# Softmax over 32,768 columns: five unequal pieces scaled on two engines, and a first load that ends in sixteen narrow transfers

## The chip, the cores and the metric

The kernel runs on one core of a Trainium2 chip. The metric is the device time of one execution in microseconds. The kernel before takes 2512.25 us, the median of three runs (2511.07 to 2513.49).

## The reference

A softmax over the last axis of a float32 tensor of 16 x 256 x 32768 (4096 rows of 32,768 columns, 537 MB in and as much out), with temperature 1.0:

```python
scaled = logits / temperature
scaled = scaled - scaled.max(axis=-1, keepdims=True)
exp_scaled = np.exp(scaled)
return exp_scaled / exp_scaled.sum(axis=-1, keepdims=True)
```

## The kernel before

Each row is cut into two halves of 16,384 columns, and the halves are laid on neighbouring partitions. A tile is 128 such half rows: 64 KB on each partition, 8.4 MB. There are 64 tiles and three tile buffers in one SBUF tensor `xs` (tile g uses buffer g mod 3). Every element is read from HBM once and written once.

All data moves through one queue, issued by SyncE (SP). `transfers` (L61) writes the order out by hand. "L" is a load and "S" a store of a tile: loads of tiles 0, 1 and 2; store 0 and load 3, each in two halves; stores 1 and 2; then for every following tile its load and the store of the tile before; at the end the loads of tiles 62 and 63, the stores of 61 and 62, and the last store in quarters. SP waits before a load until the store that last used the buffer has landed (L211), and before a store until the tile is scaled (L220). A transfer once issued stands in the queue behind those before it.

The work on one tile is in `compute` (L120). It cuts the tile into K = 4 pieces of `_PIECE` = 4096 columns. For each piece:

- VectorE takes the negative maximum of the piece per partition into a column of `t` (L133).
- ScalarE replaces the piece by exp(x - piece maximum) and adds up the exponentials into another column of `t` (L146).

Then come the small steps on 128 x 8 elements: VectorE swaps neighbouring partitions so that each half row sees the figures of the other half (L157), takes the maximum of the row (L161); ScalarE computes the factors exp(piece maximum - row maximum) into `ee` (L168); VectorE sums the row (L174) and takes the reciprocal (L186). At last VectorE multiplies each piece in place by its factor and the reciprocal in one instruction (L193), and the tile can be stored. The small tensors `t`, `ee`, `junk` and `row` exist twice (tile parity), so that VectorE waits, before it begins a tile, for the small steps of the tile before the last.

`Stream.wait` and `Stream.done` (L24, L34) set waits and increments of the engines; `Lanes.add` (L49) gives transfers their semaphores.

Of the kernel before, what the change touches and what calls it, by code (L numbers as in the profile page):

```python
# [7 lines left out]

_W = 16384
_BUFS = 3  # L10
_PIECE = 4096
_LAST_STORE = 4096


class Stream:


    def __init__(self, nc, engine, name):
        self.engine = engine
        self.sem = nc.alloc_semaphore(name)  # L20
        self.count = 0
        self.seen = {}
# [38 lines left out]
def transfers(n):  # L61
    half = _W // 2
    whole = [(0, _W)]
    halves = [(0, half), (half, half)]
    quarters = [(s, _LAST_STORE) for s in range(0, _W, _LAST_STORE)]
    plan = [("L", 0, whole), ("L", 1, whole), ("L", 2, whole)]
    plan += [("S", 0, halves), ("L", 3, halves), ("S", 1, whole), ("S", 2, whole)]
    for i in range(4, n - 2):
        plan += [("L", i, whole), ("S", i - 1, whole)]
    plan += [("L", n - 2, whole), ("L", n - 1, whole)]  # L70
    plan += [("S", n - 3, whole), ("S", n - 2, whole), ("S", n - 1, quarters)]
    return plan


@with_exitstack
def kernel(
    ctx: ExitStack,
    tc: tile.TileContext,
    logits: bass.AP,
    temperature: bass.AP,  # L80
    out: bass.AP,
):
    nc = tc.nc
    inv_t = 1.0 / float(temperature)
    P = nc.NUM_PARTITIONS
    fp32 = mybir.dt.float32
    Exp = mybir.ActivationFunctionType.Exp
    A = mybir.AluOpType

    xf = logits.flatten_outer_dims()  # L90
    of = out.flatten_outer_dims()
    N, V = xf.shape
    assert V == 2 * _W and (N * 2) % P == 0
    x = xf.rearrange("n (h v) -> (n h) v", h=2)
    o = of.rearrange("n (h v) -> (n h) v", h=2)
    G = N * 2 // P
    K = _W // _PIECE
    swap = [i ^ 1 for i in range(32)]

    ctx.enter_context(tc.tile_critical())  # L100
    X = nc.alloc_sbuf_tensor("xs", [P, _BUFS * _W], fp32)
    T = [nc.alloc_sbuf_tensor(f"t{q}", [P, 4 * K], fp32) for q in range(2)]
    E = [nc.alloc_sbuf_tensor(f"ee{q}", [P, 2 * K], fp32) for q in range(2)]
    J = [nc.alloc_sbuf_tensor(f"junk{q}", [P, 2 * K], fp32) for q in range(2)]
    R = [nc.alloc_sbuf_tensor(f"row{q}", [P, 4], fp32) for q in range(2)]

    sp = Stream(nc, nc.sync, "sp")
    dve = Stream(nc, nc.vector, "dve")
    act = Stream(nc, nc.scalar, "act")
    loads = Lanes(nc, "ld")  # L110
    stores = Lanes(nc, "st")
    landed = {}
    stored = {}
    scaled = {}
    hist = {}

    def overlapping(parts, s, n):
        return [token for (a, m), token in parts.items() if a < s + n and s < a + m]

    def compute(g):  # L120
        base = (g % _BUFS) * _W
        t, e, j_, r = T[g % 2], E[g % 2], J[g % 2], R[g % 2]
        tv = t[:, 0 : 4 * K].rearrange("p (a b k) -> p a b k", a=2, b=2)
        old = hist.get(g - 2)
        if old:
            dve.wait(*old)
        sums = None
        for k in range(K):
            s = k * _PIECE
            xs = X[:, base + s : base + s + _PIECE]  # L130
            dve.wait(*overlapping(landed[g], s, _PIECE))
            m = dve.done(
                nc.vector.tensor_reduce(  # L133
                    out=t[:, k : k + 1], in_=xs, axis=mybir.AxisListType.X, op=A.max, negate=True
                )
            )
            if inv_t != 1.0:
                dve.wait(m)
                m = dve.done(
                    nc.vector.tensor_scalar_mul(  # L140
                        out=t[:, k : k + 1], in0=t[:, k : k + 1], scalar1=inv_t
                    )
                )
            act.wait(m)
            sums = act.done(
                nc.scalar.activation(  # L146
                    out=xs,
                    in_=xs,
                    func=Exp,
                    bias=t[:, k : k + 1],  # L150
                    scale=inv_t,
                    accum_out=t[:, K + k : K + k + 1],
                )
            )
        dve.wait(sums)
        sh = dve.done(
            nc.vector.stream_shuffle(out=t[:, 2 * K : 4 * K], in_=t[:, 0 : 2 * K], mask=swap)  # L157
        )
        dve.wait(sh)
        mx = dve.done(  # L160
            nc.vector.tensor_reduce(  # L161
                out=r[:, 0:1], in_=tv[:, :, 0, :], axis=mybir.AxisListType.XY, op=A.min
            )
        )
        act.wait(mx)
        ev = e[:, 0 : 2 * K].rearrange("p (a k) -> p a k", a=2)
        ee = act.done(
            nc.scalar.activation(  # L168
                out=ev, in_=tv[:, :, 0, :], func=Exp, bias=r[:, 0:1], scale=-1.0
            )  # L170
        )
        dve.wait(ee)
        tr = dve.done(
            nc.vector.tensor_tensor_reduce(  # L174
                out=j_[:, 0 : 2 * K].rearrange("p (a k) -> p a k", a=2),
                in0=ev,
                in1=tv[:, :, 1, :],
                scale=1.0,
                scalar=0.0,
                op0=A.mult,  # L180
                op1=A.add,
                accum_out=r[:, 1:2],
            )
        )
        dve.wait(tr)
        rc = dve.done(nc.vector.reciprocal(out=r[:, 2:3], in_=r[:, 1:2]))  # L186
        dve.wait(rc)
        scaled[g] = {}
        for k in range(K):
            s = k * _PIECE  # L190
            xs = X[:, base + s : base + s + _PIECE]
            scaled[g][s, _PIECE] = dve.done(
                nc.vector.tensor_scalar(  # L193
                    out=xs,
                    in0=xs,
                    scalar1=e[:, k : k + 1],
                    scalar2=r[:, 2:3],
                    op0=A.mult,
                    op1=A.mult,
                )  # L200
            )
        hist[g] = (ee, tr)

    for what, g, parts in transfers(G):
        base = (g % _BUFS) * _W
        rows = slice(g * P, (g + 1) * P)
        if what == "L":
            landed[g] = {}
            for k, (s, n) in enumerate(parts):
                if g >= _BUFS:  # L210
                    sp.wait(*overlapping(stored[g - _BUFS], s, n))  # L211
                landed[g][s, n] = loads.add(
                    (g % _BUFS, k),
                    nc.sync.dma_start(out=X[:, base + s : base + s + n], in_=x[rows, s : s + n]),
                )
            compute(g)
        else:
            stored[g] = {}
            for k, (s, n) in enumerate(parts):
                sp.wait(*overlapping(scaled[g], s, n))  # L220
                stored[g][s, n] = stores.add(
                    (g % _BUFS, k),
                    nc.sync.dma_start(out=o[rows, s : s + n], in_=X[:, base + s : base + s + n]),  # L223
                )
    sp.wait(*stores.tokens())
# [35 lines left out]
```

## Time and profile before

| | |
|---|---|
| median of 3 runs | 2512.25 us |
| profiled execution | 2513.76 us |
| its span, first to last instruction | 2512.0 us |
| VectorE busy | 1755.7 us (70%) |
| ScalarE busy | 993.5 us (40%) |
| the transfer queue: share of 16 DMA engines' span | 99.8% |
| read from and written to HBM | 536.87 MB each |
| mean rate over the span | 427 GB/s |

The span is what the profile's views cover; 1.8 us of the execution lie outside it. DVE is VectorE, ACT is ScalarE, SPq the queueing of transfers by SyncE. The share of the queue adds up the durations of all packets; a packet is what one of the 16 DMA engines moves for one row of a transfer, 64 KB for a load or store of a whole tile. Engine idle times are named with what released the engine.

### The profile page before, as it was taken

The page shows a single profiled execution, that of the slowest core. Times are in us where ns is not written, and L with a number is a line of the kernel's source. Part 1 is how long each engine was busy: PE and PEld are TensorE (multiplying, and loading weights), DVE is VectorE, ACT ScalarE, POOL GpSimd, SP SyncE. Part 2 cuts the span into 40 slices and gives each one's busy share as a digit, 9 for nine tenths or more (in the row PEclk, how much of TensorE's full clock was granted, in tenths as well). Part 3 has the DMA queues.
Part 4 walks back from the last instruction along what each step waited for, and adds up shares of the span by engine and source line. Part 5 has one row for each costly group of instructions (what it writes and reads, how often), then busy time and mean ns, then how long its engine had stood idle before and what let it go on. Part 6 is the DMA issues. An engine that isn't in the chain of part 4 may idle for free.

```text
span 2512.0 us, 1661 instructions
## 1 busy us (share of the span) xinstructions
DVE 1755.7 (70%) x896; ACT 993.5 (40%) x577; POOL 0.2 (0%) x4
## 2 busy tenths in 40 slices
DVE  5866676766767667677676766777767676676776
ACT  3443342433424334243342433424334244342443
POOL 0000000000000000000000000000000000000000
DMA  9999999999999999999999999999999999999999
GB/s 409 443 427 432 434 432 432 425 432 432 420 433 425 429 431 422 432 424 430 433 421 431 434 427 425 434 431 422 433 432 421 431 422 433 433 420 432 434 420 389
DMA packets 19165, 1073.86 MB, mean 427 GB/s; under 512 B 2128, under 2 KB 2128, under 8 KB 2128
## 3 DMA queue, kind: packets, MB, share of 16 engines
q1 hardware_dynamic: 19152, 1073.75, 99.8%
q14 instruction: 13, 0.11, 0.0%
HBM read 536.87 MB, written 536.87 MB: 427 GB/s over the span
## 4 chain that ended last, share of the span: by engine, by line
DMA 57%; DVE 36%; ACT 5%; SPq 0%; issue 0%
DMA xs<-in_logits_dram 56%; DVE t L133 23%; DVE xs L193 12%; ACT xs L146 5%; DMA out_dram<-xs 1%; ACT ee L168 0%; SPq L223 0%; DVE row L186 0%; DVE row L161 0%; DVE t L157 0%; DVE junk L174 0%; DVE row L174 0%; SPq L256 0%; SPq L100 0%
## 5 line engine op out<-in xcount | busy, mean ns | idle before, releaser
L146 ACT ACTIVATE xs<-xs,t 128x4096 f32<-128x4096 f32 x256 | 949.2, 3708 | 1464.4 <-DVE t L133 1464.4
L133 DVE TENSOR_REDUCE t<-xs 128x1 f32<-128x4096 f32 x256 | 1113.4, 4412 | 462.1 <-DMA xs<-in_logits_dram 462.1
L193 DVE TENSOR_SCALAR xs<-xs,ee,row 128x4096 f32<-128x4096 f32 x256 | 600.4, 2409 | 2.3
L157 DVE LOAD_MASK_SELECT t<-t x64 | 0.9, 14 | 248.1 <-ACT xs L146 248.1
L146 ACT ACTIVATION_READ_ACCUMULATOR xs<-xs,t 128x1 f32 x256 | 47.7, 186 | 0.0
L168 ACT ACTIVATE ee<-t,row 128x8 f32<-128x8 f32 x64 | 19.2, 301 | 27.6 <-DVE row L161 27.6
L174 DVE CUSTOM_DVE_ANT_1 junk<-ee,t 128x8 f32<-128x8 f32 x64 | 10.7, 167 | 23.6 <-ACT ee L168 23.6
L186 DVE RECIPROCAL row<-row 128x1 f32<-128x1 f32 x64 | 10.5, 164 | 2.2
L161 DVE TENSOR_REDUCE row<-t 128x1 f32<-128x8 f32 x64 | 10.3, 161 | 2.2
L157 DVE STREAM_SHUFFLE t<-t 128x8 f32<-128x8 f32 x64 | 10.2, 160 | 0.0
L174 DVE DVE_READ_ACCUMULATOR2_ANT row<- 128x1 f32 x64 | 5.3, 83 | 0.0
L146 ACT ACT_TABLE_LOAD x1 | 1.3, 1283 | 0.9 <-SPq L100 0.9
L242 POOL MEMSET const-bfloat16-1.0<- 128x1 bf16 x1 | 0.1, 101 | 0.0
L242 POOL MEMSET const-uint8-127<- 128x1 uint8 x1 | 0.1, 101 | 0.0
L242 POOL MEMSET const-float32-0.0<- 128x1 f32 x1 | 0.1, 98 | 0.2 <-issue 0.2
L242 POOL MEMSET const-float32-1.0<- 128x1 f32 x1 | 0.1, 98 | 0.0
## 6 DMA issues: line engine op xcount, KB each, us to landing
out_dram<-xs SPq DMA_DIRECT2D x2, 4096.0 KB, 25.1
xs<-in_logits_dram SPq DMA_DIRECT2D x2, 4096.0 KB, 19.3
out_dram<-xs SPq DMA_DIRECT2D x4, 2048.0 KB, 10.8
xs<-in_logits_dram SPq DMA_DIRECT2D x63, 46.1
out_dram<-xs SPq DMA_DIRECT2D x62, 26.7
```

Of the source, the lines that this page charges most:

```text
L133: nc.vector.tensor_reduce(out=t[:, k : k + 1], in_=xs, axis=mybir.AxisListType.X, op=A.max, negate=True)
L146: nc.scalar.activation(out=xs, in_=xs, func=Exp, bias=t[:, k : k + 1], scale=inv_t, accum_out=t[:, K + k : K + k + 1],)
L157: nc.vector.stream_shuffle(out=t[:, 2 * K : 4 * K], in_=t[:, 0 : 2 * K], mask=swap)
L161: nc.vector.tensor_reduce(out=r[:, 0:1], in_=tv[:, :, 0, :], axis=mybir.AxisListType.XY, op=A.min)
L168: nc.scalar.activation(out=ev, in_=tv[:, :, 0, :], func=Exp, bias=r[:, 0:1], scale=-1.0)
L174: nc.vector.tensor_tensor_reduce(out=j_[:, 0 : 2 * K].rearrange("p (a k) -> p a k", a=2), in0=ev, in1=tv[:, :, 1, :], scale=1.0, scalar=0. ...
L186: rc = dve.done(nc.vector.reciprocal(out=r[:, 2:3], in_=r[:, 1:2]))
L193: nc.vector.tensor_scalar(out=xs, in0=xs, scalar1=e[:, k : k + 1], scalar2=r[:, 2:3], op0=A.mult, op1=A.mult,)
L242: nc = _bacc.Bacc("TRN2", target_bir_lowering=False, num_devices=1)
```

## The change

- A tile has five pieces of 4096, 4096, 4096, 2560 and 1536 columns instead of four of 4096. The small steps work on 128 x 10 elements.
- A new small VectorE multiplication joins the factor of each piece with the reciprocal. Then the pieces are scaled by this one factor: pieces 2 and 3 (4096 and 2560 columns) on ScalarE, pieces 0, 1 and 4 (4096, 4096 and 1536) on VectorE.
- VectorE's wait before it begins a tile also covers the scalings of the tile before the last.
- Tile 0 is loaded as 15,360 columns in one transfer, and the last 1024 columns in 16 transfers. Each of these moves 8 partitions, every fourth one in a group of 32. All 16 count on one semaphore. They stand in the queue between the wide load of tile 0 and the load of tile 1.

The code is split into methods of a class `Tile` (`exponentials`, `totals`, `scale`), which `compute` calls one after the other. The order of the other transfers is as before.

```diff
-_PIECE = 4096
+_PIECES = (4096, 4096, 4096, 2560, 1536)
+_ON_ACT = (2, 3)
 _LAST_STORE = 4096
+_NARROW = 1024
...
-    plan = [("L", 0, whole), ("L", 1, whole), ("L", 2, whole)]
+    wide = [(0, _W - _NARROW)]
+    plan = [("L", 0, wide), ("N", 0, [(_W - _NARROW, _NARROW)]), ("L", 1, whole), ("L", 2, whole)]
...
-        for k in range(K):
-            s = k * _PIECE
-            xs = X[:, base + s : base + s + _PIECE]
-            scaled[g][s, _PIECE] = dve.done(
-                nc.vector.tensor_scalar(
-                    out=xs,
-                    in0=xs,
-                    scalar1=e[:, k : k + 1],
-                    scalar2=r[:, 2:3],
-                    op0=A.mult,
-                    op1=A.mult,
-                )
-            )
-        hist[g] = (ee, tr)
...
+            hist[self.g] = (ee, tr)
+
+        def scale(self):
+            f = self.j
+            w = dve.done(
+                nc.vector.tensor_scalar_mul(out=f[:, 0:K], in0=self.e[:, 0:K], scalar1=self.r[:, 2:3])
+            )
+            act.wait(w)
+            dve.wait(w)
+            for k in range(K):
+                xs = self.piece(k)
+                if k in _ON_ACT:
+                    token = act.done(nc.scalar.mul(out=xs, in_=xs, mul=f[:, k : k + 1]))
+                else:
+                    token = dve.done(
+                        nc.vector.tensor_scalar_mul(out=xs, in0=xs, scalar1=f[:, k : k + 1])
+                    )
+                scaled[self.g][starts[k], _PIECES[k]] = token
+            hist[self.g] += tuple(scaled[self.g].values())
...
+            if what_next != "N":
+                compute(g)
+        elif what == "N":
+            s, n = parts[0]
+            for q in range(0, P, 32):
+                for j in range(4):
+                    some = slice(q + j, q + 32, 4)
+                    landed[g][s, n] = loads.add(
+                        ("n",),
+                        nc.sync.dma_start(
+                            out=X[some, base + s : base + s + n],
+                            in_=x[g * P + q + j : g * P + q + 32 : 4, s : s + n],
+                        ),
+                    )
             compute(g)
```

More of the change, by code (lines that the diff above doesn't have):

```diff
@@ L96 @@
     G = N * 2 // P
-    K = _W // _PIECE
+    K = len(_PIECES)
+    starts = [sum(_PIECES[:k]) for k in range(K)]
+    assert sum(_PIECES) == _W
     swap = [i ^ 1 for i in range(32)]
@@ L118, in overlapping, with __init__, piece, exponentials @@
         return [token for (a, m), token in parts.items() if a < s + n and s < a + m]
[L120 to L127, printed above, removed]
-        for k in range(K):
-            s = k * _PIECE
-            xs = X[:, base + s : base + s + _PIECE]
-            dve.wait(*overlapping(landed[g], s, _PIECE))
+    class Tile:
+        def __init__(self, g):
+            self.g = g
+            self.base = (g % _BUFS) * _W
+            self.t, self.e, self.j, self.r = T[g % 2], E[g % 2], J[g % 2], R[g % 2]
+            self.tv = self.t[:, 0 : 4 * K].rearrange("p (a b k) -> p a b k", a=2, b=2)
+            self.sums = None
+            scaled[g] = {}
+        def piece(self, k):
+            s = self.base + starts[k]
+            return X[:, s : s + _PIECES[k]]
+        def exponentials(self, k):
+            t = self.t
+            if k == 0 and self.g >= 2:
+                dve.wait(*hist[self.g - 2])
+            xs = self.piece(k)
+            dve.wait(*overlapping(landed[self.g], starts[k], _PIECES[k]))
             m = dve.done(
@@ L144, in compute @@
             act.wait(m)
-            sums = act.done(
+            self.sums = act.done(
                 nc.scalar.activation(
@@ L154, in compute @@
             )
-        dve.wait(sums)
-        sh = dve.done(
-            nc.vector.stream_shuffle(out=t[:, 2 * K : 4 * K], in_=t[:, 0 : 2 * K], mask=swap)
-        )
[L159 to L162, printed above, removed]
-            )
-        )
[L165 to L179, printed above, removed]
-                op0=A.mult,
[L181 to L191, printed above, removed]
-            scaled[g][s, _PIECE] = dve.done(
-                nc.vector.tensor_scalar(
-                    out=xs,
-                    in0=xs,
-                    scalar1=e[:, k : k + 1],
-                    scalar2=r[:, 2:3],
-                    op0=A.mult,
-                    op1=A.mult,
-                )
-            )
-        hist[g] = (ee, tr)
@@ L204, with totals @@
-    for what, g, parts in transfers(G):
+        def totals(self):
+            t, e, r, tv = self.t, self.e, self.r, self.tv
+            dve.wait(self.sums)
+            sh = dve.done(
+                nc.vector.stream_shuffle(out=t[:, 2 * K : 4 * K], in_=t[:, 0 : 2 * K], mask=swap)
+            )
+            dve.wait(sh)
+            mx = dve.done(
+                nc.vector.tensor_reduce(
+                    out=r[:, 0:1], in_=tv[:, :, 0, :], axis=mybir.AxisListType.XY, op=A.min
+                )
+            )
+            act.wait(mx)
+            ev = e[:, 0 : 2 * K].rearrange("p (a k) -> p a k", a=2)
+            ee = act.done(
+                nc.scalar.activation(
+                    out=ev, in_=tv[:, :, 0, :], func=Exp, bias=r[:, 0:1], scale=-1.0
+                )
+            )
+            dve.wait(ee)
+            tr = dve.done(
+                nc.vector.tensor_tensor_reduce(
+                    out=self.j[:, 0 : 2 * K].rearrange("p (a k) -> p a k", a=2),
+                    in0=ev,
+                    in1=tv[:, :, 1, :],
+                    scale=1.0,
+                    scalar=0.0,
+                    op0=A.mult,
+                    op1=A.add,
+                    accum_out=r[:, 1:2],
+                )
+            )
+            dve.wait(tr)
+            rc = dve.done(nc.vector.reciprocal(out=r[:, 2:3], in_=r[:, 1:2]))
+            dve.wait(rc)
+            hist[self.g] = (ee, tr)
@@ new lines, in scale @@
+        def scale(self):
+            f = self.j
+            w = dve.done(
+                nc.vector.tensor_scalar_mul(out=f[:, 0:K], in0=self.e[:, 0:K], scalar1=self.r[:, 2:3])
+            )
+            act.wait(w)
+            dve.wait(w)
+            for k in range(K):
+                xs = self.piece(k)
+                if k in _ON_ACT:
[3 more added lines that the diff above has]
+                        nc.vector.tensor_scalar_mul(out=xs, in0=xs, scalar1=f[:, k : k + 1])
+                    )
+                scaled[self.g][starts[k], _PIECES[k]] = token
+            hist[self.g] += tuple(scaled[self.g].values())
@@ L205, with compute @@
+    def compute(g):
+        a = Tile(g)
+        for k in range(K):
+            a.exponentials(k)
+        a.totals()
+        a.scale()
+    plan = transfers(G)
+    for (what, g, parts), (what_next, _, _) in zip(plan, plan[1:] + [(None, None, None)]):
         base = (g % _BUFS) * _W
@@ L215 @@
                 )
+            if what_next != "N":
[11 more added lines that the diff above has]
+                        ),
+                    )
             compute(g)
```

## The prediction

> **What bounds the kernel now.** I read the page first: is any compute engine full, or is it the transfers?
>
> ```profile
> DVE 1755.7 (70%) x896; ACT 993.5 (40%) x577; POOL 0.2 (0%) x4
> ...
> GB/s 409 443 427 432 434 432 432 425 432 432 420 433 425 429 431 422 432 424 430 433 421 431 434 427 425 434 431 422 433 432 421 431 422 433 433 420 432 434 420 389
> ...
> q1 hardware_dynamic: 19152, 1073.75, 99.8%
> ```
>
> No engine is full; the one queue has packets in flight for 99.8% of 16 engines' span. The best slices run at 434 GB/s, and many stand at 420 to 425. 1073.75 MB at 434 GB/s is 2474 us, so of the span of 2512.0 us some 35 us can be lost at most. Where? The windows, cut to fractions of a packet, tell it. GB/s counts a packet (one 65,536-byte row of one DMA engine) where it starts, so packets = GB/s x width / 65.536, and the mean duration of a packet = DMA share x width x 16 / packets.
>
> ```profile
> core 0: us, DVE busy (x) ACT busy (x) POOL busy (x), PEclk, DMA share, GB/s
> 14.50:15.20 0.70, 0.00 (x0) 0.00 (x0) 0.00 (x0) 1.00 3.45 1498
> 58.10:58.80 0.70, 0.70 (x2) 0.00 (x0) 0.00 (x0) 1.00 4.97 1498
> 156.10:157.40 1.30, 0.00 (x0) 0.00 (x0) 0.00 (x0) 1.00 2.13 706
> 349.70:350.40 0.70, 0.00 (x0) 0.00 (x0) 0.00 (x0) 1.00 2.38 1030
> 351.70:352.20 0.50, 0.00 (x0) 0.00 (x0) 0.00 (x0) 1.00 0.76 262
> ```
>
> At 14.5 us all 16 engines start a packet together and take 2.42 us for it (3.45 x 0.7 x 16 / 16): the undisturbed pace, a tile's transfer in 19.32 us. At 58.1 us, the last packets of tile 2's load before the first store, all 16 take 3.48 us: 1.06 lost. At 156.1 us (last load packets of tile 4, 14 of them) 3.16: 0.75 lost. At 349.7 us only 11 engines start tile 9's last load packet together, and take 2.42: nothing lost. Two of the five behind them start theirs at 351.7 to 352.2 and take 3.04 (0.76 x 0.5 x 16 / 2): 0.62 lost. In the packet records nearly all that is lost up to 450 us lies in this last packet of a load, before the engine turns to a store. (Later the engines in front lose too, since their stores are issued only after the slowest engine's landing; that does not move the slowest.) So engines that are ahead turn free, those behind pay, and a landing counts when the slowest engine is in. Now the chain:
>
> ```profile
> 350.05 45.66 DMA xs<-in_logits_dram
> 395.73 17.41 DVE t L133 x4
> ...
> 418.14 9.39 DVE xs L193 x4
> 427.55 0.33 SPq L223
> ```
>
> Landing to store issue takes 31.8 us (395.73 to 427.55); then 45.8 us of queueing and loading. It looks as if compute shared the bound. It doesn't: the 45.8 us are mostly another store and load ahead in the queue. Two tiles are 77.3 us of transfers alone (4 x 19.32), and the chain takes 78.3 on average: landings 161.73 (tile 4) to 2432.70 (tile 62), 58 tiles, 39.155 us each against 38.64. So 0.515 us is lost per tile, 30 us in all, by the engines behind. A store is issued about 38.64 - 31.8 = 6.8 us before the slowest engine has need of it.
>
> **The change, part by part.** Sums stand against the profiled execution: 2513.76 us, span 2512.0. The median of the runs is 1.5 us less.
>
> *Compute.*
>
> ```profile
> L146 ACT ACTIVATE xs<-xs,t 128x4096 f32<-128x4096 f32 x256 | 949.2, 3708 | 1464.4 <-DVE t L133 1464.4
> L133 DVE TENSOR_REDUCE t<-xs 128x1 f32<-128x4096 f32 x256 | 1113.4, 4412 | 462.1 <-DMA xs<-in_logits_dram 462.1
> L193 DVE TENSOR_SCALAR xs<-xs,ee,row 128x4096 f32<-128x4096 f32 x256 | 600.4, 2409 | 2.3
> ...
> L168 ACT ACTIVATE ee<-t,row 128x8 f32<-128x8 f32 x64 | 19.2, 301 | 27.6 <-DVE row L161 27.6
> ```
>
> ACT pays 3708 ns for 4096 columns and 301 for 8, so 0.294 us and 0.833 per 1000 columns: 2.43 us for 2560 columns, 1.57 for 1536. VectorE's reduction by the same line against the 161 ns one: 2.8 and 1.75. Landing to the scale factor is 22.4 us now (395.73 to 418.14). Five reductions end 0.15 later, but ScalarE, still behind with the third and fourth exponential (to 17.0 and 19.6), ends the fifth at 21.4 instead of 21.2; one more small multiply is 0.17 plus a hop of 0.1 to 0.2 (rows of 128x8): 22.9. Then scaling runs on both: VectorE 2 x 2.35 + 1.0 = 5.7, ScalarE 3.71 + 2.43 = 6.1 instead of 9.4. The store is issued at 29.1: 2.7 us sooner. Scaling on ScalarE is not in the trace; its price is taken from the exponential (same size), and one function set is loaded in the program as before. Both engines stay below the 39.1 us of a tile (VectorE 24, ScalarE 23). Gain on the path: 0, because the queue is never empty on the slowest engine. Without that cover it would be 2.7 per tile. At the end the last tile's stores (issued from 2489.2) come sooner, which helps engines that wait there since 2485.7, not the slowest: it leaves the store before at 2491.0.
>
> *Waits.* VectorE's wait on the previous user of its scratch now includes the scalings of two tiles ago: over 30 us past. VectorE and ScalarE wait for the factor (0.17); behind it stand only this tile's scalings. 0.
>
> *The narrow load.* It takes 1024 columns, 4 KB a row, 0.5 MB, from tile 0's load. SyncE issues 16 more transfers at 0.38 to 0.47 us (start to start of the three loads at 0.95, 1.38, 1.85 us): 7 us, so tile 1's load is issued at 8.5 instead of 1.4, with the wide load running to 20.6. Hidden. A transfer of 8 rows can use at most eight engines, since a packet is one row. If these are always the same eight, each of them carries 16 x 4 = 64 KB here and the other eight nothing (evenly it would be 32 KB each): from the first tile on eight engines are one packet, 2.41 us, behind the other eight. No row shows an 8-row transfer; bounds for this offset are 0 (they alternate) and 2.41; I take 2.41, since all 16 are alike. Their own finish is 32 KB later than with an even load: 1.2 us.
>
> The Trainium skill, DMA: Bandwidth & Descriptors, "Why a DMA increments its semaphore by 16 and not by 1", states that such a transfer takes the largest count up to 16 that divides the rows, on the lowest-numbered engines: always the same eight. No row here shows it.
>
> What does the offset do to the turns? With 16 engines turning together they lost 1.06 and 0.75, mean 0.9; with 10 or 11 in front, those behind lose 0.515 per tile. Along that line, 0.07 per engine in front, eight in front cost 0.33. That is an estimate from two points. Bounds: 0 (those in front at 350 us pay nothing) to 0.9. Sum: 0.185 x 60 = 11.1 gained, 2 x 0.5 in the two joint turns, less 1.2: 11 us. 2513.8 - 11 = 2502.8, at the median **2501.5**.
>
> **The rivals.** *Halves turn free:* eight in front and eight a whole packet behind never disturb each other, and nothing is lost but start and offset: 30 + 2 less 1.2, or 2481.5. For it: those in front lost nothing in some 16 turns from 160 to 450 us. Against: those behind, by up to 5 us, did.
>
> *Earlier stores cost (slower):* the loss may come with a store that stands in the queue before the last load packet begins. By rows: ends 2.1 to 4.5 us after the issue lose nothing (in front), about 6.5 us 0.5 (behind), 8.8 to 11 us 0.75 and 1.06 (all engines; issues at 149.68 and 49.94). With stores 2.7 us sooner the slowest ends at 9.3, about 0.85: 0.33 more on 60 tiles, 20 us: 2532. It decides once the engines in front exceed some 5 us too. Against: at 100 us a store 14 us early cost next to nothing.
>
> *Nothing moves:* the offset isn't there or dissolves, and the loss is what it was: 2508 to 2516.
>
> *Narrow transfers in single file:* 1.0 us each from issue (0.95) to first packet (1.96), 16 us once, on the critical engines: 2527. Against: a queued load follows the one before with no gap here (rounds of 2.42 us go on past 21.8 us).
>
> The Trainium skill, same page, "Rules for kernel authors", speaks against the change: under 64 KB a transfer is mostly overhead. With its fixed 2 us each the first tile would end 32 us later.
>
> **How the numbers follow.** Less offset loss as worked out: 0.32. Halves free: 0.18. Earlier stores: 0.30. Nothing moves: 0.15. Single file: 0.05. 0.2% is 5 us, about what a measurement can tell. Faster takes 0.30 of the first and the second, 0.48; same 0.02 and 0.13; slower 0.02, 0.30 and 0.05. The forecast's own range is 2494 to 2509; the whole reaches from the free halves (2480) to the dearer turns (2531).
>
> **What would show it.** The offset: windows of 0.7 us with eight starts, then none, then eight, in tile after tile. The turns: last load packets at 2.42 in both halves (free) or near 2.75 (forecast) or above 3.2 (rival). Tile to tile 38.97 us instead of 39.155. Landing to issue 29.1. I am wrong if engines are again eleven and five, if the first tiles lose over 10 us, or if the time moves with the issue alone.

## The result: 21 us faster

| | before | after |
|---|---|---|
| median | 2512.87 us (4 runs) | 2491.86 us (4 runs, 2491.0 to 2492.49) |
| profiled execution | 2513.76 us | 2491.0 us |
| its span | 2512.0 us | 2489.2 us |

The ratio is 0.9915, 95% interval 0.9901 to 0.9929. The forecast was 2501.5 us in a range of 2480 to 2531: the direction was right and the gain twice as large as forecast. The result lies below 2494 to 2509, the range that the forecast gave to its own reckoning.

### The profile page after: what moved, and what is told of

It reads as the page before. It is cut to its first block, busy times and chain, and to the rows that moved or that the text cites. A ratio compares the mean times of both kernels' runs of the same rounds, so it can differ in the third digit from the quotient of the medians.

```text
span 2489.2 us, 2061 instructions
## 1 busy us (share of the span) xinstructions
DVE 1529.5 (61%) x960; ACT 1390.4 (56%) x833; POOL 0.2 (0%) x4
## 3 DMA queue, kind: packets, MB, share of 16 engines
q1 hardware_dynamic: 19408, 1073.75, 99.8%
## 4 chain that ended last, share of the span: by engine, by line
DMA 60%; DVE 19%; ACT 18%; another core or an unknown queue 1%; issue 0%; SPq 0%
DMA xs<-in_logits_dram 57%; DVE t L146 17%; ACT xs L159 10%; ACT xs L216 7%; DMA out_dram<-xs 3%; DVE xs L219 1%; ACT ee L184 0%; SPq L265 0%; DVE junk L209 0%; DVE row L202 0%; DVE row L177 0%; DVE t L173 0%; DVE junk L190 0%; DVE row L190 0%
## 5 line engine op out<-in xcount | busy, mean ns | idle before, releaser
L146 DVE TENSOR_REDUCE t<-xs 128x1 f32<-128x4096 f32 (+2 forms) x320 | 1117.3, 3558 | 681.3 <-DMA xs<-in_logits_dram 681.3
L159 ACT ACTIVATE xs<-xs,t 128x4096 f32<-128x4096 f32 (+2 forms) x320 | 965.9, 3019 | 1000.7 <-DVE t L146 1000.7
L216 ACT ACTIVATE xs<-xs,junk 128x4096 f32<-128x4096 f32 (+1 forms) x128 | 385.9, 3062 | 45.5 <-DVE junk L209 45.5
L219 DVE TENSOR_SCALAR xs<-xs,junk 128x4096 f32<-128x4096 f32 (+1 forms) x192 | 354.9, 1906 | 2.3
L159 ACT ACTIVATION_READ_ACCUMULATOR xs<-xs,t 128x1 f32 x320 | 59.6, 186 | 0.0
L184 ACT ACTIVATE ee<-t,row 128x10 f32<-128x10 f32 x64 | 19.5, 305 | 27.9 <-DVE row L177 27.9
L190 DVE CUSTOM_DVE_ANT_1 junk<-ee,t 128x10 f32<-128x10 f32 x64 | 10.9, 170 | 23.8 <-ACT ee L184 23.8
L209 DVE TENSOR_SCALAR junk<-ee,row 128x5 f32<-128x5 f32 x64 | 14.8, 231 | 2.2
L177 DVE TENSOR_REDUCE row<-t 128x1 f32<-128x10 f32 x64 | 10.5, 164 | 2.2
L173 DVE STREAM_SHUFFLE t<-t 128x10 f32<-128x10 f32 x64 | 10.4, 162 | 0.0
## 6 DMA issues: line engine op xcount, KB each, us to landing
out_dram<-xs SPq DMA_DIRECT2D x2, 4096.0 KB, 29.2
```

The source lines that it names most:

```text
L146: nc.vector.tensor_reduce(out=t[:, k : k + 1], in_=xs, axis=mybir.AxisListType.X, op=A.max, negate=True)
L159: nc.scalar.activation(out=xs, in_=xs, func=Exp, bias=t[:, k : k + 1], scale=inv_t, accum_out=t[:, K + k : K + k + 1],)
L177: nc.vector.tensor_reduce(out=r[:, 0:1], in_=tv[:, :, 0, :], axis=mybir.AxisListType.XY, op=A.min)
L184: nc.scalar.activation(out=ev, in_=tv[:, :, 0, :], func=Exp, bias=r[:, 0:1], scale=-1.0)
L190: nc.vector.tensor_tensor_reduce(out=self.j[:, 0 : 2 * K].rearrange("p (a k) -> p a k", a=2), in0=ev, in1=tv[:, :, 1, :], scale=1.0, scala ...
L209: nc.vector.tensor_scalar_mul(out=f[:, 0:K], in0=self.e[:, 0:K], scalar1=self.r[:, 2:3])
```

## The profile after

The lines of the page that answer to those shown of before, and the row of the queue that fetches instructions:

```profile
DVE 1529.5 (61%) x960; ACT 1390.4 (56%) x833; POOL 0.2 (0%) x4
...
GB/s 411 439 432 429 438 437 434 426 436 437 428 434 437 437 429 432 438 434 434 431 436 436 436 428 436 438 433 432 433 438 432 429 437 435 432 431 438 430 429 368
...
q1 hardware_dynamic: 19408, 1073.75, 99.8%
q14 instruction: 17, 0.14, 0.0%
```

The share of the queue is 99.8% as before, because it adds up how long packets take, including those that take too long. The GB/s row is the better guide. A packet counts where it starts, and 16 that start nearly together are 1 MB of the 27 MB of a slice, so that neighbouring slices differ by a few per cent; the mean of slices 2 to 39 is 433.7 here and was 429.1. An undisturbed packet is 65,536 bytes in 2.418 us, which is 433.7 GB/s on 16 engines. So on the mean of the engines next to nothing is lost any more.

The turn of tile 9's load, in windows like those of before (starts of packets = GB/s x width / 65.536):

```profile
core 0: us, DVE busy (x) ACT busy (x) POOL busy (x), PEclk, DMA share, GB/s
348.00:348.70 0.70, 0.00 (x0) 0.00 (x0) 0.00 (x0) 1.00 2.81 1217
348.70:350.70 2.00, 0.00 (x0) 0.00 (x0) 0.00 (x0) 1.00 0.30 131
350.70:351.80 1.10, 0.00 (x0) 0.00 (x0) 0.00 (x0) 1.00 2.06 894
```

13 packets start in the first window, 4 in the second and 15 in the third, and they take 2.42, 2.40 and 2.42 us each (2.81 x 0.7 x 16 / 13, 0.30 x 2.0 x 16 / 4, 2.06 x 1.1 x 16 / 15). By the packet records the last packets of the load are in the first window on the eight engines in front, and in the third on the eight behind. Before, two of the five engines behind took 3.04 here. Now the chain:

```profile
655.68 48.43 DMA xs<-in_logits_dram
...
704.13 13.09 DVE t L146 x3
...
717.24 7.78 ACT xs L159 x6
...
726.47 6.04 ACT xs L216 x2
...
732.96 0.33 SPq L265
```

From the start of VectorE on the landed tile at 704.1 to the end of scaling at 732.5 are 28.4 us, against 31.8 before; the store is issued at once or, as here, up to 0.45 us later. From landing to landing the chain takes 38.758 us per tile: tile 4 lands at 161.30 and tile 62 at 2409.29, and 2247.99 / 58 is that. Before it was 39.155. The loss per tile on the slowest engine fell from 0.515 to 0.118 us: 58 x 0.397 = 23.0 us, and the spans differ by 22.8.

## Two theories, and what the packet records add

Two parts of the change could have done this: the narrow transfers, which set eight engines one packet behind the others, and the faster work between landing and store. The forecast gave everything to the first.

The packet records hold 16 ends for every transfer, one of each engine, so one can follow how far the last engine lies behind the first (called its **lag** here). Before, the lag begins at 0.6 us, and grows by some 0.4 per tile until it is 5 to 6 us, at about 500 us. By then the engines in front have caught up with the compute: their next store is issued too late for them, and the loss goes on to the end. Their **time in hand** is what a tile's transfers take, less the time from landing to issue, less the lag: 38.64 - 31.8 = 6.8 us less the lag before, 38.64 - 28.4 = 10.2 us less the lag now.

After, eight engines end tile 1 within 0.4 us and the other eight 2.6 to 2.7 us behind the first; from 119 us on the last is 3.5 behind. From 60 to 440 us next to nothing is lost at the turns, one turn at 464 us costs all 16 engines 0.69 (mean), and then next to nothing is lost until 1836 us. In this loss-free state the last engine still falls behind, in jumps:

| 8 KB packet of the instruction queue starts (us) | lag before it and after it (us) |
|---|---|
| 769.0 | 4.88, 5.73 |
| 1117.6 | 5.74, 6.68 |
| 1444.5 | 6.68, 7.48 |
| 1776.1 | 7.48, 8.43 |
| 2103.1 | 7.88, 8.65 |

Of the 6.8 us that the slowest engine loses in all between tiles 4 and 62 (58 x 0.118), these five jumps are 4.3.

At a lag of 8.4, with 10.2 - 8.4 = 1.8 us in hand, the engines in front begin to wait and losses return. What this waiting is can be read from the store of tile 46, its issue and the stretch in which its last packets start on the engines in front:

```profile
1818.08 0.33 SPq L265 DMA_DIRECT2D out_dram<-xs  x1
...
1836.20:1836.75 0.55, 0.55 (x1) 0.34 (x2) 0.00 (x0) 1.00 1.54 596
```

The store is issued at 1818.08 us, and by the packet records the first engine is done with its load at 1819.37. No gap opens: it starts on the store at once. But the five packets of the window take 2.71 us on average (1.54 x 0.55 x 16 / 5) instead of 2.42, and the first engine ends the store at 1839.14, which is 21.06 us after the issue, or 19.32 + 1.74. Two more stores of this run lose over 0.15 us in this way, and the first engine ends them 19.32 + 1.73 and 19.32 + 1.76 us after their issue; in the kernels below that lose much, the median is mostly 1.7. So "waiting" means here that the issue comes less than some 1.7 us before the first engine needs it, and that this engine then ends the store later by what is missing. Why that falls mostly on the last packet the records do not tell. Real gaps between an engine's packets add up to 2.0 us per engine before and 0.5 now (200 to 2380 us); the last packets of stores lose 13.3 us per engine before and 0.3 now, those of loads 7.1 and 1.5.

The theory is then: **time in hand** carries the gain. While the engines in front never wait, the engines settle into a spread in which no turn costs anything; the offset only gives them this spread from the start. The rival is the forecast's: **the offset** alone makes the turns cheap.

## The experiments

The ratios are against runs of the kernel before on the same chip. In the expectations, theory 1 is the offset, theory 2 the earlier stores, and theory 3 that both are needed.

### One part of the change at a time

*The offset alone*: the kernel before, with the narrow transfers of the change.

```diff
--- before
-    plan = [("L", 0, whole), ("L", 1, whole), ("L", 2, whole)]
+    wide = [(0, _W - _NARROW)]
+    plan = [("L", 0, wide), ("N", 0, [(_W - _NARROW, _NARROW)]), ("L", 1, whole), ("L", 2, whole)]
...
```

> The kernel before with the 16 narrow transfers alone (four pieces, scaling on VectorE). Theory 1 (the offset of one packet between two groups of eight engines makes the turns from load to store free): about 2491, as the changed kernel, perhaps 2 to 3 us less since it has fewer instructions; 0.7 us windows show eight starts, none, eight. Theory 2 (the stores issued 3 us sooner bring the gain): 2510 to 2514. Theory 3 (both are needed, since with stores issued late the engines in front run out of work): 2498 to 2508.

Measured 2516.04 us (10 runs), ratio 1.0008 (0.9999 to 1.0018). The page's rate tells how long the offset helps:

```profile
GB/s 409 434 432 434 434 425 427 434 432 420 433 429 423 434 423 431 433 432 420 434 425 427 434 428 424 434 426 426 434 427 425 434 423 429 434 422 430 434 418 395
```

A slice is 62.8 us. Slices 2 to 5 stand at 432 to 434, then 425, 427 and 420 come in as before. In the packet records the lag is 4.0 us at 255 us, with 2.8 in hand. At 272 us a turn costs the last engine 0.5, the next two 1.0 and 0.8; from 350 us on nearly every store is issued less than 1.7 us before the first engine needs it, and the lag stays below 6.4 while losses go on. The offset is there, and but for one turn at 156 us (0.9 on the mean of the engines) the turns are free, for 270 of 2500 us. All three expectations were below the measured time.

*The pieces alone*: the kernel after, with tile 0 loaded whole.

```diff
--- after
-    wide = [(0, _W - _NARROW)]
-    plan = [("L", 0, wide), ("N", 0, [(_W - _NARROW, _NARROW)]), ("L", 1, whole), ("L", 2, whole)]
+    plan = [("L", 0, whole), ("L", 1, whole), ("L", 2, whole)]
```

> The changed kernel with tile 0 loaded whole in one transfer. Theory 1: no gain, 2508 to 2516, and if earlier stores cost (the rival of the prediction) up to 2532. Theory 2: about 2491. Theory 3: 2508 to 2516.

Measured 2506.15 us (2497.05 to 2509.27, 6 runs), ratio 0.9964 (0.9948 to 0.9980). The time lies between the expectations: below the 2508 to 2516 of theories 1 and 3, far above the 2491 of theory 2. The lag grows from 0.6 to some 9 us at 1120 us, by 0.3 to 0.4 per tile, at turns that cost the engines behind although for the first 970 us the stores are issued 1.9 us or more ahead; then the engines in front begin to wait and the losses stay. So the faster work alone gains some 6 us by the medians (9 by the ratio), the offset alone nothing, and both together 21.

*The same 1024 columns as one transfer of 128 partitions*, so that all engines carry the same:

```diff
--- after
-            for q in range(0, P, 32):
-                for j in range(4):
...
+            landed[g][s, n] = loads.add(
+                ("n",),
+                nc.sync.dma_start(out=X[:, base + s : base + s + n], in_=x[rows, s : s + n]),
+            )
```

> The changed kernel with the last 1024 columns of tile 0 in one transfer of 128 partitions: the cut is there, but every engine gets 32 KB of it and no offset arises. Theory 1: as without the cut, 2508 to 2532, all engines start packets together at first. If only the cut of the first load mattered (tile 0 starting sooner): about 2491.

Measured 2506.12 us (2491.87 to 2510.17, 10 runs), ratio 0.9969 (0.9954 to 0.9984), as the pieces alone. It is the uneven load that counts, not the cut. One run of ten came out at 2492, where all four runs of the changed kernel are.

### The size of the offset

```diff
--- after; half a packet
-_NARROW = 1024
+_NARROW = 512
--- after; two packets
-_NARROW = 1024
+_NARROW = 2048
```

> The changed kernel with 512 narrow columns: the groups are half a packet (1.2 us) apart. If any split in two groups of eight frees the turns: about 2490 to 2492. If the engines behind pay as soon as they are over 1 us late (as in the kernel before), with 0.33 us a tile: about 2503. If the groups must be a whole packet apart so that one group's last packet doesn't meet the other's turn: 2500 to 2512.

> The changed kernel with 2048 narrow columns: the groups are two packets (4.8 us) apart. Theory 3a: the turns are free at first, but the engines in front have 2.4 us less in hand (about 4 instead of 6.4), so the free state ends sooner, by 700 to 1000 us instead of 1836: 2496 to 2506. If only the grouping matters: 2493.

Half: 2498.9 us (2491.56 to 2510.78, 10 runs), ratio 0.9955 (0.9937 to 0.9972). The offset in the profiled run was 1.8 us, and that run, 2510.78, lost from 158 us on. Since the ten runs scatter over 19 us, this kernel does not tell its three expectations apart: half a packet is enough in some runs and not in others. Two packets: 2507.8 us (10 runs), ratio 0.9971 (0.9961 to 0.9980), 2 us above what was expected of it. Its rate:

```profile
GB/s 402 435 435 435 435 435 435 434 433 435 435 435 433 429 427 435 433 429 427 434 431 423 435 430 427 429 433 423 430 425 431 425 429 426 430 425 429 435 421 370
```

Slices 2 to 13 (to 815 us) lose nothing, and nearly every pair behind them does. With an offset of twice the size, the lag is 5.9 us at 215 us and passes 7.8 at 790 us. A larger offset spends the time in hand at the start.

### The time in hand

The next kernels keep the offset and change the time from landing to issue.

```diff
--- after; all scaling on VectorE
-_ON_ACT = (2, 3)
+_ON_ACT = ()
--- after; one piece on ScalarE
-_ON_ACT = (2, 3)
+_ON_ACT = (3,)
--- after; four pieces, the third on ScalarE
-_PIECES = (4096, 4096, 4096, 2560, 1536)
-_ON_ACT = (2, 3)
+_PIECES = (4096, 4096, 4608, 3584)
+_ON_ACT = (2,)
--- after; no scaling of the pieces
-                xs = self.piece(k)
-                if k in _ON_ACT:
...
+                token = w
```

> The changed kernel (five pieces, offset) with all five pieces scaled on VectorE. Landing to store issue becomes about 32 us instead of 28.4, as in the kernel before; all else is as changed. Theory 3a (the offset frees the turns only as long as the engines in front get their store 2.5 us or more before they need it): 2510 to 2518, as with the offset alone, good for the first 300 us and then lost. Theory 3b (it was the five pieces or the work on ScalarE, not the latency): about 2492.

> The changed kernel with only the piece of 2560 columns scaled by ScalarE; VectorE scales the other four. Landing to store issue is some 30.3 us instead of 28.4, so the engines in front have 8.3 us in hand less some 1.4 that they need: a lag of 6.9. Theory (time in hand sets when the free state ends): the lag reaches 6.9 at about 1450 us instead of 1836, and then 0.4 to 0.5 us are lost per tile on some 27 tiles: 2496 to 2504, between the 2492 at 28.4 us and the 2515 at 31.6. Rival (it is not the time in hand but which engine scales, or a threshold): either 2492 or 2512 to 2516.

> The changed kernel with four pieces (4096, 4096, 4608, 3584) instead of five, the third scaled by ScalarE. It tells what the fifth piece is worth. Landing to store issue should be some 29.4 us, the cap on the lag 7.8, and VectorE has 14 instead of 15 instructions per tile. Theory: the free state ends at about 1780 us: 2492 to 2497. Rival (five pieces matter by themselves): 2500 or more.

> The changed kernel with the scaling of the pieces left out (the factor is still computed): landing to issue about 22.5 us, so the engines in front have 6 us more in hand. Theory 3a: the free state holds to the end, 2480 to 2487, with only the engine that falls behind singly (8 KB instruction fetches) setting the end. If a store that stands long in the queue costs (rival of the prediction): 2500 or more.

| landing to issue (us) | in hand without lag (us) | losses return at (us) | median (us) | ratio, interval |
|---|---|---|---|---|
| 31.6 (all on VectorE) | 7.0 | 235, at a lag of 4.1 | 2515.11 | 1.0005, 0.9995 to 1.0014 |
| 30.2 (one piece) | 8.4 | about 1160, at 6.5 | 2503.33 | 0.9957, 0.9941 to 0.9974 |
| 29.2 (four pieces) | 9.4 | about 1930, at 7.8 | 2493.26 | 0.9918, 0.9903 to 0.9933 |
| 28.4 (the change) | 10.2 | 1836, at 8.4 | 2491.86 | 0.9915, 0.9901 to 0.9929 |
| 22.5 (no scaling) | 16.1 | never at the end; some from 313 to 1440 | 2489.06 | 0.9903, 0.9888 to 0.9918 |

The time follows the time in hand, step by step. With one piece on ScalarE the losses returned sooner than expected (1160 us, not 1450), with four pieces later (1930, not 1780); both medians lie in the expected ranges. In the three middle rows 1.6 to 1.9 us are still in hand when losses return. In the first row it is 2.9, and 2.8 with the offset alone, so that late stores do not explain the first turns that lose there. With one piece on ScalarE the page shows the state ending in the middle of a run:

```profile
GB/s 410 436 436 435 435 434 435 427 433 435 436 435 436 435 436 436 432 429 429 435 429 435 427 429 434 425 429 425 433 421 433 423 423 434 421 434 433 423 420 379
```

Slices are 62.6 us here. Slices 2 to 16, up to 1001 us, have a mean of 434.7, and slices 17 to 39 one of 428.5. The fifth piece by itself is worth nothing that can be measured (the ratios of four and five pieces overlap). The kernel without scaling (it leaves out a part of the softmax) came out 2 us above what was expected: it too loses at some turns, although its engines in front never wait.

*No offset and no scaling*: the two edits shown, together.

> The same without scaling and without the offset (tile 0 loaded whole). Theory 3a (both are needed): the engines lose at the turns from the start, 2500 to 2510. If time in hand alone sufficed: 2480 to 2487 as with the offset.

Measured 2490.89 us (2488.37 to 2491.64, 4 runs), ratio 0.9912 (0.9896 to 0.9929): both expectations missed, the first by 9 us and the second by 4, and the miss of the first tells most. Without any offset this kernel loses for some 700 us while its engines drift apart, to about 1, 4 and 5 us behind; then next to nothing is lost at the turns to the end. So the spread forms by itself if there is time in hand enough. The offset is worth 14 us at 28.4 us (2506.15 to 2491.86; 12 by the ratios), and 2 at 22.5.

### What ends the loss-free state

Fifteen more VectorE instructions per tile, behind the scalings, in time that VectorE has free:

```diff
--- after
+            for _ in range(_EXTRA):
+                x_ = dve.done(nc.vector.reciprocal(out=self.r[:, 3:4], in_=self.r[:, 2:3]))
+                dve.wait(x_)
```

> The changed kernel, and behind the scalings of each tile 15 small VectorE instructions (reciprocals of 128 x 1 into a column that nothing reads). They start after the store is released and last some 3.5 us of the 10 us that VectorE has free there, so landing to store issue stays at 28.4 us. VectorE's instructions per tile double from 15 to 30. Theory (one engine falls behind by 0.7 to 0.95 us at each 8 KB packet of the instruction queue that belongs to VectorE, seven times in the run, and the loss-free state ends when its lag reaches some 8.4 us): the packets come every 165 us instead of every 330, the lag reaches 8.4 us before 1100 us instead of at 1836, and from there 0.4 to 0.5 us are lost per tile: 2498 to 2508. Rival (the lag grows by something else, by time or by turns): the free state ends at about 1836 us as before, 2490 to 2494.

Measured 2502.4 us (2502.22 to 2503.66, 4 runs), ratio 0.9959 (0.9944 to 0.9974). The page, with the group of the added line:

```profile
GB/s 411 436 436 435 435 433 432 427 436 436 436 434 435 435 436 434 431 430 434 435 426 431 434 430 428 434 428 425 434 432 424 433 428 429 430 425 424 434 421 367
...
q14 instruction: 25, 0.20, 0.0%
```

```profile
L225 DVE RECIPROCAL row<-row 128x1 f32<-128x1 f32 x960 | 157.6, 164 | 30.5
```

The added work is 2.5 us per tile of VectorE (157.6 / 64), behind the store's release, and the store is issued as early as before. The instruction packets rose from 17 to 25. In the packet records six of them start at 243.0, 398.4, 553.7, 709.1, 864.4 and 1041.5 us, and just there the lag goes from 3.4 to 4.2, 5.0, 5.8, 6.5, 7.3 and 8.3. Up to then the turns are free (slices 2 to 17, to 1063 us, have a mean of 434.2); from 1100 us on losses are back (slices 18 to 39: 429.5), as they were from 1836 us with packets half as often. So it is shown that these fetches make the last engine late, by 0.8 to 0.95 us each, and that the loss-free state ends when its lag has used up all but some 2 us of the time in hand (10.2 - 8.3).

### More time in hand by another route

Loads of tiles 4 to 61 in two halves, so that work on the first half starts before the second has landed:

```diff
--- after
-        plan += [("L", i, whole), ("S", i - 1, whole)]
+        plan += [("L", i, halves), ("S", i - 1, whole)]
```

> The changed kernel with the loads of tiles 4 to 61 in two transfers of 8192 columns, so that the first three pieces' work begins half a load earlier. After the second half has landed there are the reductions of 4096, 2560 and 1536 columns, their exponentials, the small steps and the scaling: some 19.7 us to the store issue instead of 28.4, the cap on the lag some 17.5 us. Theory (time in hand): the slowest engine's lag of 8 to 9 us at the end never reaches the cap, and nothing is lost after the first joint turns but the instruction packets: 2482 to 2489. Rival (loss comes with each transfer's end, or with smaller packets): twice the transfers cost up to 0.5 us more per tile, 2500 to 2520.

Measured 2492.99 us (2492.89 to 2493.1, 4 runs), ratio 0.9920 (0.9906 to 0.9935): no better than the change, 4 us above what was expected. The chain:

```profile
665.94 4.43 DVE t L146
...
670.40 7.78 ACT xs L159 x6
...
679.61 6.04 ACT xs L216 x2
```

From the second half's landing to the end of scaling it takes 19.7 us (665.94 to 685.65), as worked out, and the packet records show what the theory asks for: from 30 us on and until the last stores, no turn loses more than a few hundredths of a us in the mean of its engines, and the lag goes up to 9.7 us at the end without anyone waiting. But the stores follow one another by 38.70 and later 38.79 us instead of 38.64. Packets of 32 KB take 1.213 us, 4 ns more than half of 2.418, and a tile's load has 16 of them per engine: 0.06 per tile, 3.7 us in 58 tiles. The other 0.09, in the later part, belongs to one engine that falls behind a little at every tile; its cause was not looked for.

No kernel that computes the whole softmax came out below the changed one.

## Why the prediction was right, and where its steps failed

That the forecast came out right is in good part luck. It gave the whole gain to the offset, and the offset alone gave none: 2516.04 us, where the forecast's sum for it is 2501.5. What made the offset count is the faster work, which the sum has at 0. One of the forecast's own signs of being wrong did show: with the offset kept, the time moved with the issue alone, from 2515.11 us at 31.6 to 2489.06 at 22.5.

**What bounds the kernel** stood: the transfers, with the loss at the turns of the engines behind.

**The offset** was costed at 2.41 us and measured at 2.6 to 2.75 between the groups. That one half of the engines is spared shows where the wide load ends:

```profile
core 0: us, DVE busy (x) ACT busy (x) POOL busy (x), PEclk, DMA share, GB/s
20.20:21.40 1.20, 0.00 (x0) 0.00 (x0) 0.00 (x0) 1.00 1.59 529
21.40:23.20 1.80, 1.57 (x1) 0.00 (x0) 0.00 (x0) 1.00 0.54 178
23.20:25.20 2.00, 2.00 (x1) 0.00 (x0) 0.00 (x0) 1.00 1.65 571
```

The first window moves 635 KB: eight packets of 64 KB (tile 1, on the engines in front) and 27 narrow ones of 4 KB. The second moves 320 KB, narrow packets alone; in the third all 16 engines start a large one. So the trace agrees with the Trainium skill (DMA: Bandwidth & Descriptors, "Why a DMA increments its semaphore by 16 and not by 1") that the 16 transfers use the same eight engines.

**The turns** were the term that was mis-sized. A line through 16, and 10 to 11, engines in front gave 0.33 us per tile; the chain shows 0.118, and the packet records nothing at nearly every turn up to 1836 us. How many engines are in front is not what sets it: with the same eight in front, and 31.6 or 31.8 us from landing to issue, the loss was as large as before. The rival *Halves turn free* had the right turns for most of the run (2481.5 us), but for a reason that isn't enough, and without the instruction packets and the losses behind 1836 us.

**"Gain on the path: 0, because the queue is never empty on the slowest engine"** is the step that failed. The sentence is true of the slowest engine. But the engines in front did get their stores too late, from about 500 us on, and the profile had the number: 6.8 us from the store's issue to the slowest engine's need, with engines 5 us ahead of it. The forecast set that aside with "that does not move the slowest". The runs speak against that: where the engines in front wait for long, the slowest loses 0.4 to 0.6 us per tile too (0.44 with the added VectorE instructions from 1093 us on, 0.57 with one piece on ScalarE from 1169 on, 0.515 before). An estimated 0.1 to 0.2 of it comes from instruction fetches, at 0.8 us every 4 to 8 tiles. In the changed kernel's last 600 us, with little waiting, the slowest loses some 0.1 in all. Why their waiting costs the others at the turn was not settled, nor why engines that run close together lose; the runs show only that both are so.

**The work from landing to issue** was costed at 29.1 us and took 28.4 (up to 28.85 to the issue): the factor comes at 22.3 us instead of 22.9, and the scaling on ScalarE takes 6.04 instead of 6.1. The groups:

```profile
L216 ACT ACTIVATE xs<-xs,junk 128x4096 f32<-128x4096 f32 (+1 forms) x128 | 385.9, 3062 | 45.5 <-DVE junk L209 45.5
L219 DVE TENSOR_SCALAR xs<-xs,junk 128x4096 f32<-128x4096 f32 (+1 forms) x192 | 354.9, 1906 | 2.3
...
L209 DVE TENSOR_SCALAR junk<-ee,row 128x5 f32<-128x5 f32 x64 | 14.8, 231 | 2.2
```

**The narrow issues** cost SP more than the 0.38 to 0.47 us each of the forecast. The timeline of SP:

```profile
0.96 0.38 SPq L242 DMA_DIRECT2D xs<-in_logits_dram  x1
1.39 10.79 SPq L253 DMA_DIRECT2D xs<-in_logits_dram  x16
12.22 0.92 SPq L242 DMA_DIRECT2D xs<-in_logits_dram  x2
```

10.79 / 16 is 0.67 us each, and tile 1's load is issued at 12.2 instead of 8.5; the wide load still hides it. *Narrow transfers in single file* is refuted: up to 22.6 us most of the 4 KB packets take 159 ns each, later ones up to 340, and all have ended by 24.5 us. The Trainium skill's rule (same page, "Rules for kernel authors") is that under 64 KB a transfer is mostly overhead. The forecast's estimate of 32 us takes sixteen times in a row the fixed 2 us that the Trainium skill, in the same page, fits to transfers issued by GpSimd. The trace does not bear the estimate out: the narrow columns and tile 1 follow the wide load without a gap. The overhead that the trace does show is the 0.67 us of SP for each.

**Earlier stores cost** (2532 us) is refuted: stores now stand in the queue some 9.7 us before the slowest engine needs them, and next to nothing is lost. **Nothing moves** is what the offset does without the faster work (2516.04 us).

**What would show it** had one bad pointer: the windows of eight starts, none, and eight. An offset of 2.6 us is nearly a packet of 2.42, so that the two groups start within a few tenths of each other, one packet apart. The starts of packets hide the offset; only the ends of transfers show it.

## What to carry to other kernels

Where one queue feeds all DMA engines, work out the time in hand of the engine in front, not only of the slowest: the pace of the queue, less the time from landing to the next issue, less how far the last engine lies behind. Shorter compute can pay there although no engine waits for it on the critical path, and two edits that are worth 0 and 6 us alone can be worth 21 together. Read the rate over the slices of the run: a state that holds for a while and then ends shows there, when totals and shares show nothing.

## What the runs showed that was not expected

- A fetch of 8 KB of instructions (309 ns by its record) makes the last engine 0.8 to 0.95 us later in the loss-free state, by the fetch itself and by a longer packet right behind it. At 15 VectorE instructions per tile such a fetch comes every 310 to 350 us, at 30 every 155 to 180.
- A transfer of 8 partitions takes SP 0.67 us to issue, one of a whole tile some 0.4.
- A store that is issued too late for the engines in front mostly leaves no gap: its last packet is longer. A busy share of 99.8% does not show it.
- The same kernel without a clear offset ends anywhere between 2492 and 2510 us from run to run (1024 columns in one even transfer); with an offset of one packet and 28.4 us from landing to issue it stayed within 1.5 us in four runs.
